# Two-block transformer kernel: the modulation's context sums by one VectorE instruction each

## The chip, the cores and the metric

One core of one Trainium2 chip runs the whole program; nothing is shared with other cores. The metric is the time of one execution in microseconds (us) of device time. The engines are named as in the profile: PE is TensorE's matmuls and PEld its weight loads, DVE is VectorE, ACT is ScalarE, POOL is GpSimd and SP is the engine whose queue issues most transfers.

## The reference, cut to what matters

The input passes through two blocks of two layers each. The first block has in each layer a gated feed-forward network, an attention mixer and a second such network; the second block has attention over image and context tokens and a feed-forward network. What the change touches is the modulation of the second block. For each of its two layers `l`, two vectors of 1024 numbers (the silu of `c` and the silu of `c_ctx`) are multiplied by one matrix:

```
sc = jax.nn.silu(c)
sc_ctx = jax.nn.silu(c_ctx)
mod   = split_cols((sc     @ w_mod[l] + b_mod[l])[:, None, :], (D_MODEL,) * N_MOD)
mod_x = split_cols( sc_ctx @ w_mod[l] + b_mod[l],              (D_MODEL,) * N_MOD)
```

`w_mod[l]` is 1024 x 6144 in float32, 25 MB a layer. Both products need only the inputs, so they can be computed at any time before the second block uses them.

## The kernel before, in words

**Main work.** Everything large is a matmul in three passes (`mm3`, lines 335 to 343): weights and activations are each split into a rounded high part and a rest, and high by high, low by high and high by low are added up in PSUM. The weights come as 539 tiles of 128 x 1024 float32, in the order in which they are used (class `Weights`). Each tile is loaded by SP's queue into one of 3 staging buffers (`wst`, line 274). ScalarE copies it to a rounded high part (`whi`, line 295) and VectorE subtracts that from the tile to get the rest (`wlo`, line 296). There are 4 buffers each of `whi` and `wlo`, and a tile is split 4 tiles ahead of its use (line 305). A tile holds 8 blocks of 128 x 128, so it feeds 24 matmuls.

**The feed-forward layers of the first block** (`ffn1_layer`, lines 871 to 912). An up phase has 22 steps; each multiplies two blocks of columns (48 matmuls, two weight tiles), then VectorE scales the result (896) and multiplies it by its silu (899), and ScalarE and VectorE split the product for the next phase (347, 348). A down phase has 8 steps of 66 matmuls, each with an eviction by VectorE (830), and the input of the next layer split by ScalarE (542) and VectorE (543) while POOL adds up squares (556). After each step of either phase `self.step()` (350) takes one step of every background generator. What a background step issues is tied behind the step's last split and last matmul, so that it does not come ahead of these in the queues. The order of each engine's queue beyond that is set when the program is built, by a scheduler that works through a simulated time line.

**The modulation** (`mod_gen`, lines 722 to 796) is such a generator. It runs beside the first three feed-forward layers for layer 0 (`w_mod` in 6 chunks of 1024 columns, two chunks to each feed-forward layer), and beside the feed-forward network of the second block's first layer for layer 1 (12 chunks of 512 columns). For a chunk, 8 tiles `mw` of 128 x CW are loaded one after another by SP's queue (737). For each, `n` sums are kept in `macc`: number 0 belongs to `c` and number 1 to the context. The tile times one of the 16 columns of `sc` (a number for each partition) is added to its sum. For the first tile ScalarE writes both products (751). For the other seven, number 0 is multiplied and added by VectorE in one instruction (753). Number 1 is multiplied by ScalarE into a buffer `mp` (756, two buffers), and POOL adds that to `macc` (757). In layer 1 number 1 is only needed for 4 of the 12 chunks. Then ones-matmuls on TensorE add over the partitions (769), and the rows go by DRAM to where they are used. This makes 6 x 7 = 42 additions of 1024 columns and 4 x 7 = 28 of 512 columns for number 1, and 42 and 12 x 7 = 84 for number 0.

Beside the second feed-forward layer another generator (`later_gen`, line 464) prepares constants by VectorE (479 to 524) and with two small matmuls (483, 509).

Of the kernel before, what the change touches and what calls it, by code (L numbers as in the profile page):

```python
# [8 lines left out]
FT = mybir.dt.float32  # L9
FR = mybir.dt.float32r  # L10
I32 = mybir.dt.int32
AF = mybir.ActivationFunctionType
OP = mybir.AluOpType
# [296 lines left out]
class Body:  # L310
# [411 lines left out]
    def mod_gen(self, pool, l, c0, c1, CW, nb, wait=0):  # L722

        nc = self.nc
        for _ in range(wait):
            yield
        gs = list(range(c0, c1, CW))
        if l:
            gs = gs[4:8] + gs[:4] + gs[8:]
        todo = [(g, k) for g in gs for k in range(KB)]  # L730
        ws = []

        def load():
            if todo:
                g, k = todo.pop(0)
                ws.append(pool.tile([128, CW], FT, name="mw", bufs=nb))
                nc.sync.dma_start(ws[-1], self.a["wmod"][l, k * 128:(k + 1) * 128, g:g + CW])

        for _ in range(nb - 1):
            load()  # L740
        yield
        for g in gs:
            n = 2 if l == 0 or g < 2 * D else 1
            acc = pool.tile([128, 2, CW], FT, name="macc")
            for k in range(KB):
                load()
                w = ws.pop(0)
                for i in range(n):
                    s = self.sc[:, i * 8 + k:i * 8 + k + 1]
                    if k == 0:  # L750
                        nc.scalar.activation(acc[:, i], w, AF.Copy, scale=s)
                    elif i == 0:
                        nc.vector.scalar_tensor_tensor(acc[:, i], w, s, acc[:, i], op0=OP.mult, op1=OP.add)  # L753
                    else:
                        t = pool.tile([128, CW], FT, name="mp", bufs=2)
                        nc.scalar.activation(t, w, AF.Copy, scale=s)  # L756
                        nc.gpsimd.tensor_tensor(acc[:, i], acc[:, i], t, op=OP.add)  # L757
                if CW == 1024 or k == KB - 1:
                    yield
                if CW == 1024 and k in (2, 5):  # L760
                    yield
            yield
            if CW == 1024:
                yield
            w = CW * n // 4
            rows = [(i, c) for i in range(n) for c in range(0, CW, w)]
            ps = self.ps("st")
            for p, (i, c) in enumerate(rows):
                nc.tensor.matmul(ps[32 * p:32 * p + 32, :w], self.ones[:, :32], acc[:, i, c:c + w], start=True,
                                 stop=True, tile_position=(0, 32 * p), skip_group_check=True)  # L770
            mr = self.w2(1)[:, 0, :w]
            nc.scalar.activation(mr, ps[:, :w], AF.Copy)
            for p, (i, c) in enumerate(rows):
                nc.sync.dma_start(self.rowd[l][i:i + 1, g + c:g + c + w], mr[32 * p:32 * p + 1])
            yield
        if c1 == 6 * D:
            mt = pool.tile([128, CW], FT, name="mt", tag="mp", bufs=2)[:96, :128]
            if n == 2:
                nc.sync.dma_start(mt, self.rowd[l].rearrange("i (k c) -> (i k) c", c=128))
            else:  # L780
                nc.vector.memset(mt, 0.0)
                nc.sync.dma_start(mt[:48], self.rowd[l][0:1].rearrange("i (k c) -> (i k) c", c=128))
                nc.sync.dma_start(mt[48:64], self.rowd[l][1:2, :2048].rearrange("i (k c) -> (i k) c", c=128))
            yield
            ps = self.ps("st")
            nc.tensor.transpose(ps[:, :96], mt, self.ident[:96, :96])
            b = self.vec[:, _VEC["b_mod"] + 48 * l:_VEC["b_mod"] + 48 * l + 48]
            mv = self.modv[l].rearrange("p (i c) -> p i c", i=2)
            nc.vector.tensor_tensor(mv, ps[:, :96].rearrange("p (i c) -> p i c", i=2),
                                    b[:, None, :].to_broadcast([128, 2, 48]), op=OP.add)  # L790
            for half in range(2):
                c = 24 * half + 16
                nc.vector.tensor_scalar(mv[:, :, c:c + 8], mv[:, :, c:c + 8], 1.0 / ALPHA, None, op0=OP.mult)
                nc.vector.tensor_scalar(self.s1p[l][:, :, half], mv[:, :, 24 * half + 8:24 * half + 16], 1.0, None,
                                        op0=OP.add)
            yield
# [1262 lines left out]
```

## Time and profile before

| What | us |
|---|---|
| median of 3 runs | 2051.03 |
| lowest and highest of them | 2048.58, 2056.51 |
| the profiled execution, whole | 2053.4 |
| its span, first to last instruction | 2051.6 |

The profiled execution is one run beside the three. Its time is the span and 1.8 us around it. Times in the rows are counted from the start of the span. A row's time for an instruction runs from its start to its end and includes what it was held up in between; the time that its engine stood idle ahead of it is given apart, with what released it. On TensorE matmuls overlap, so the starts are 0.12 us apart where one lasts 0.28. A time of POOL is rougher than the others.

### The profile page before, as it was taken

The numbers are of one execution on the slowest core, as the hardware profiler recorded it, in microseconds if no ns is written. First come the engines' busy times: TensorE is split into PE (matmuls) and PEld (weight loads), VectorE is DVE, ScalarE is ACT, GpSimd is POOL, SyncE is SP. The second block draws the span as 40 slices with busy tenths as digits, with TensorE's granted clock in tenths as the row PEclk, the third lists the DMA queues.
The fourth block names the chain that finished last, engine by engine and source line by source line (L and its number), as shares of the span: only waits on it lengthen the run. The fifth ranks groups of instructions, "written<-read, shape, count | busy, mean of one in ns | idle before, by whom it ended". The sixth has DMA issues, their size and how long they took to land. (4 is left out here: it accounts for less than half of the span.)

```text
span 2051.6 us, 39230 instructions
## 1 busy us (share of the span) xinstructions
PE 1985.8 (97%) x15365; PEld 1849.7 (90%) x15365; DVE 1525.1 (74%) x2683; ACT 1134.9 (55%) x2030; POOL 401.3 (20%) x305
## 2 busy tenths in 40 slices
PE   8998999998999999999999999999999999989997
PEld 8998999997999998999999777988888889869997
DVE  6887797988588867887686977766665689876554
ACT  5464586654466557555557765533443455855443
POOL 1222141312022310210430112302330014011002
PEclk9999999999999999999999999999999999999999
DMA  7775645785677663555542323475455653125553
GB/s 261 244 258 174 197 143 185 257 275 174 225 232 234 193 208 105 194 174 186 188 139 71 113 71 121 151 248 173 159 161 167 218 162 105 54 78 164 181 181 102
DMA packets 117689, 355.39 MB, mean 173 GB/s; under 512 B 21973, under 2 KB 28328, under 8 KB 117056
## 3 DMA queue, kind: packets, MB, share of 16 engines
q1 hardware_dynamic: 115904, 344.54, 51.8%
q10 hardware_dynamic: 1600, 8.36, 1.1%
q8 instruction: 120, 1.97, 0.4%
q14 instruction: 65, 0.53, 0.1%
HBM read 351.66 MB, written 8.90 MB: 176 GB/s over the span
## 5 line engine op out<-in xcount | busy, mean ns | idle before, releaser
L296 DVE TENSOR_TENSOR wlo<-wst,whi 128x1024 fp32r<-128x1024 f32 (+1 forms) x542 | 708.1, 1307 | 329.7 <-ACT whi L295 325.7
L341 PE MATMUL mm<-HI,whi 128*128 128x256 f32 (+1 forms) x2944 | 862.8, 295 | 6.8 <-ACT whi L295 2.6
L343 PE MATMUL mm<-HI,wlo 128*128 128x256 f32 (+1 forms) x2944 | 861.8, 294 | 5.8 <-DVE wlo L296 5.8
L342 PE MATMUL mm<-LO,whi 128*128 128x256 f32 (+1 forms) x2944 | 863.3, 294 | 1.5 <-DVE LO L1446 1.5
L295 ACT ACTIVATE whi<-wst 128x1024 fp32r<-128x1024 f32 (+1 forms) x542 | 569.9, 1053 | 512.4 <-PE mm L342 263.3
L341 PEld LDWEIGHTS mm<-HI,whi 128*128 128x128 f32 x2944 | 561.7, 192 | 31.1 <-issue 11.0
L343 PEld LDWEIGHTS mm<-HI,wlo 128*128 128x128 f32 x2944 | 563.5, 192 | 22.3 <-DVE wlo L296 7.4
L342 PEld LDWEIGHTS mm<-LO,whi 128*128 128x128 f32 x2944 | 564.0, 192 | 18.9 <-issue 6.0
L343 PE MATMUL mm<-ghi,wlo 128*128 128x256 f32 (+1 forms) x1000 | 290.0, 290 | 8.0 <-DVE wlo L296 8.0
L341 PE MATMUL mm<-ghi,whi 128*128 128x256 f32 (+1 forms) x1000 | 289.1, 290 | 1.6 <-ACT ghi L347 1.6
L342 PE MATMUL mm<-glo,whi 128*128 128x256 f32 (+1 forms) x1000 | 289.3, 290 | 0.6 <-DVE glo L348 0.6
L757 POOL TENSOR_TENSOR macc<-macc,mp 128x1024 f32<-128x1024 f32 (+1 forms) x70 | 162.6, 2323 | 479.5 <-ACT mp L756 332.3
L343 PEld LDWEIGHTS mm<-ghi,wlo 128*128 128x128 f32 x1000 | 193.3, 193 | 12.2 <-DVE wlo L296 8.8
L341 PEld LDWEIGHTS mm<-ghi,whi 128*128 128x128 f32 x1000 | 193.0, 193 | 6.4 <-issue 3.1
L342 PEld LDWEIGHTS mm<-glo,whi 128*128 128x128 f32 x1000 | 193.3, 193 | 3.5 <-issue 1.1
L753 DVE SCALAR_TENSOR_TENSOR macc<-mw,sc,macc 128x512 f32<-128x512 f32 (+1 forms) x126 | 175.1, 1389 | 25.1 <-DMA mw<-in_wmod 19.3
L342 PE MATMUL mm<-wlo,HI 128*128 128x256 f32 x352 | 100.5, 286 | 3.5 <-DVE wlo L296 3.5
L341 PE MATMUL mm<-whi,HI 128*128 128x256 f32 x352 | 100.9, 287 | 0.0
L343 PE MATMUL mm<-whi,LO 128*128 128x256 f32 x352 | 99.9, 285 | 0.0
L756 ACT ACTIVATE mp<-mw,sc 128x1024 f32<-128x1024 f32 (+1 forms) x70 | 67.1, 973 | 27.2 <-DMA mw<-in_wmod 18.0
L898 ACT ACTIVATE w<-w 128x256 f32<-128x256 f32 x88 | 36.1, 412 | 74.4 <-DVE w L896 73.0
L342 PEld LDWEIGHTS mm<-wlo,HI 128*128 128x128 f32 x352 | 67.5, 192 | 4.9 <-DVE wlo L296 4.1
(428 smaller groups left out, 2480.7 us busy)
## 6 DMA issues: line engine op xcount, KB each, us to landing
wst<-in_wall SPq DMA_DIRECT2D x539, 512.0 KB
mw<-in_wmod SPq DMA_DIRECT2D x48, 512.0 KB
mw<-in_wmod SPq DMA_DIRECT2D x96, 256.0 KB
brep<-bvec ACTq DMA_DIRECT2D x16, 384.0 KB
nab<-rrep SPq DMA_DIRECT2D x24, 96.0 KB
bias<-brep SPq DMA_DIRECT2D x4, 512.0 KB
bias<-brep SPq DMA_DIRECT2D x8, 256.0 KB
rrep<-in_rpb ACTq DMA_DIRECT2D x4, 348.8 KB
```

Source lines behind the costliest of these rows:

```text
L295: mark = self.nc.scalar.activation(hi[:, a:b], src[:, a:b], AF.Copy)
L296: self.nc.vector.tensor_tensor(lo[:, a:b], src[:, a:b], hi[:, a:b].bitcast(FT), op=OP.subtract)
L341: nc.tensor.matmul(ps, wh, xh, start=first, stop=False, skip_group_check=True)
L342: nc.tensor.matmul(ps, wh, xl, start=False, stop=False, skip_group_check=True)
L343: self.last = nc.tensor.matmul(ps, wl, xh, start=False, stop=last, skip_group_check=True)
L753: nc.vector.scalar_tensor_tensor(acc[:, i], w, s, acc[:, i], op0=OP.mult, op1=OP.add)
L756: nc.scalar.activation(t, w, AF.Copy, scale=s)
L757: nc.gpsimd.tensor_tensor(acc[:, i], acc[:, i], t, op=OP.add)
L898: nc.scalar.activation(sl, t[:, 0], AF.Silu)
```

## The change

For the second to eighth tile, both sums are now formed by VectorE's instruction that multiplies by a column and adds; the ScalarE product, its buffer and the POOL addition of number 1 are gone. The first tile's products stay on ScalarE. Loads, buffers of `mw` and `macc`, the generator's steps and the ones-matmuls stay as they are.

```diff
--- before.py
+++ after.py
@@ -749,12 +749,8 @@
                     s = self.sc[:, i * 8 + k:i * 8 + k + 1]
                     if k == 0:
                         nc.scalar.activation(acc[:, i], w, AF.Copy, scale=s)
-                    elif i == 0:
+                    else:
                         nc.vector.scalar_tensor_tensor(acc[:, i], w, s, acc[:, i], op0=OP.mult, op1=OP.add)
-                    else:
-                        t = pool.tile([128, CW], FT, name="mp", bufs=2)
-                        nc.scalar.activation(t, w, AF.Copy, scale=s)
-                        nc.gpsimd.tensor_tensor(acc[:, i], acc[:, i], t, op=OP.add)
                 if CW == 1024 or k == KB - 1:
                     yield
                 if CW == 1024 and k in (2, 5):
```

## Rows read from the trace of the kernel before

**Rows 1.** The page, part 1: busy time of each engine over the whole execution.

```profile
...
PE 1985.8 (97%) x15365; PEld 1849.7 (90%) x15365; DVE 1525.1 (74%) x2683; ACT 1134.9 (55%) x2030; POOL 401.3 (20%) x305
...
```

**Rows 2.** Busy time by stretch: us, engines' busy us (instructions), granted clock, DMA share, GB/s.

```profile
...
40.00:215.00 175.00, 167.41 (x1343) 161.90 (x1343) 143.33 (x144) 96.10 (x128) 44.66 (x20) 0.98 0.68 227
360.00:530.00 170.00, 160.52 (x1316) 157.76 (x1315) 143.62 (x191) 93.65 (x125) 41.15 (x18) 0.99 0.71 234
560.00:735.00 175.00, 173.68 (x1442) 171.31 (x1441) 147.36 (x150) 100.83 (x135) 46.40 (x19) 1.00 0.67 215
1330.00:1650.00 320.00, 319.35 (x1860) 270.37 (x1859) 203.64 (x255) 125.30 (x181) 44.20 (x28) 1.00 0.58 188
...
166.40:173.20 6.80, 5.47 (x25) 5.48 (x26) 6.80 (x6) 3.86 (x5) 2.73 (x2) 0.50 0.45 152
...
487.30:490.50 3.20, 3.20 (x17) 3.20 (x16) 2.63 (x4) 3.20 (x5) 1.17 (x1) 0.50 0.71 195
...
```

**Rows 3.** Waits of TensorE, 40 to 735 us: total us, times, longest.

```profile
...
PE mm L343 <- DVE wlo L296: 11.9, 7, 3.3
PE st L509 <- DVE w L499: 4.1, 1, 4.1
PE mm L341 <- ACT ghi L347: 1.6, 1, 1.6
...
```

**Rows 4.** The page, part 5: the POOL additions and the ScalarE products.

```profile
...
L757 POOL TENSOR_TENSOR macc<-macc,mp 128x1024 f32<-128x1024 f32 (+1 forms) x70 | 162.6, 2323 | 479.5 <-ACT mp L756 332.3
...
L756 ACT ACTIVATE mp<-mw,sc 128x1024 f32<-128x1024 f32 (+1 forms) x70 | 67.1, 973 | 27.2 <-DMA mw<-in_wmod 18.0
...
```

**Rows 5.** Timeline of VectorE, 157 to 169.5 us: start, us, engine, line, operation.

```profile
...
157.58 6.82 DVE L753 SCALAR_TENSOR_TENSOR macc<-mw,sc,macc 128x1024 f32<-128x1024 f32 x2
164.32 3.35 DVE L296 TENSOR_TENSOR wlo<-wst,whi 128x1024 fp32r<-128x1024 f32 x1
...
167.93 1.27 DVE L753 SCALAR_TENSOR_TENSOR macc<-mw,sc,macc 128x1024 f32<-128x1024 f32 x1
169.12 1.21 DVE L296 TENSOR_TENSOR wlo<-wst,whi 128x1024 fp32r<-128x1024 f32 x1
...
```

**Rows 6.** Timeline of POOL over the same stretch.

```profile
...
157.56 9.03 POOL L757 TENSOR_TENSOR macc<-macc,mp 128x1024 f32<-128x1024 f32 x3 [6.00 <-ACT mp L756]
...
```

**Rows 7.** Line 753 alone: instructions, shortest/median/longest in ns.

```profile
...
L753 DVE SCALAR_TENSOR_TENSOR macc<-mw,sc,macc x126: 737/754/3505, 48.1 to 1630.3; 128x512 f32<-128x512 f32 x84, 128x1024 f32<-128x1024 f32 x42
...
```

**Rows 8.** Groups of VectorE by shape, 40 to 215 us: busy us, mean ns, idle before.

```profile
...
L296 DVE TENSOR_TENSOR wlo<-wst,whi 128x1024 fp32r<-128x1024 f32 x56 | 78.3, 1401 | 26.1 <-ACT whi L295 26.1
L753 DVE SCALAR_TENSOR_TENSOR macc<-mw,sc,macc 128x1024 f32<-128x1024 f32 x14 | 30.8, 2200 | 0.0
...
```

**Rows 9.** Groups of VectorE by shape, 360 to 530 us.

```profile
...
L296 DVE TENSOR_TENSOR wlo<-wst,whi 128x1024 fp32r<-128x1024 f32 x54 | 73.8, 1368 | 24.4 <-ACT whi L295 24.4
L753 DVE SCALAR_TENSOR_TENSOR macc<-mw,sc,macc 128x1024 f32<-128x1024 f32 x14 | 33.2, 2371 | 0.0
...
L497 DVE TENSOR_SCALAR w<-vec,nbb 128x8 f32<-128x8 f32 x3 | 5.0, 1682 | 0.0
...
```

**Rows 10.** Groups of VectorE by shape, 560 to 735 us.

```profile
...
L296 DVE TENSOR_TENSOR wlo<-wst,whi 128x1024 fp32r<-128x1024 f32 x60 | 86.7, 1445 | 25.9 <-ACT whi L295 25.7
L753 DVE SCALAR_TENSOR_TENSOR macc<-mw,sc,macc 128x1024 f32<-128x1024 f32 x14 | 30.8, 2203 | 0.0
...
```

**Rows 11.** Groups of VectorE by shape, 1330 to 1650 us.

```profile
...
L753 DVE SCALAR_TENSOR_TENSOR macc<-mw,sc,macc 128x512 f32<-128x512 f32 x84 | 80.2, 955 | 25.1 <-DMA mw<-in_wmod 19.3 <-ACT macc L751 4.6
...
```

**Rows 12.** Groups of VectorE by shape, 149 to 170 us.

```profile
...
L753 DVE SCALAR_TENSOR_TENSOR macc<-mw,sc,macc 128x1024 f32<-128x1024 f32 x4 | 11.5, 2878 | 0.0
L296 DVE TENSOR_TENSOR wlo<-wst,whi 128x1024 fp32r<-128x1024 f32 x4 | 7.0, 1750 | 1.4 <-ACT whi L295 1.4
...
```

**Rows 13.** Groups of VectorE by shape, 464 to 499 us.

```profile
...
L753 DVE SCALAR_TENSOR_TENSOR macc<-mw,sc,macc 128x1024 f32<-128x1024 f32 x5 | 13.0, 2593 | 0.0
...
```

**Rows 14.** Timeline of TensorE, 160 to 168.5 us: start, us, operation, idle before.

```profile
...
167.72 0.58 PE L343 MATMUL mm<-ghi,wlo 128*128 128x256 f32 x1 [3.27 <-DVE wlo L296]
...
```


## The prediction

> **What bounds the kernel now.** I first read the busy times of the page [rows 1]: PE is busy 1985.8 of 2051.6 us, so TensorE is the bound, and another engine matters only where TensorE waits for it. VectorE, which gets the new work, is at 1525.1 us (74%), and that is an average over stages. So I read next the four stretches in which the modulation runs [rows 2]. The reader is to see that TensorE idles 175 - 167.41 = 7.6 us in the first, 9.5 in the second, 1.3 in the third and 0.6 in the fourth: 18.4 us in the three of layer 0, almost nothing in layer 1. VectorE is busy 82 to 85% of the first three and 64% of the fourth. Two short stretches run at half the clock, 6.8 us from 166.4 and 3.2 us from 487.3 [rows 2].
>
> Then I asked what TensorE waited for between 40 and 735 us [rows 3]: 11.9 us in 7 waits for the rest part of a weight tile (`wlo`, line 296), 4.1 us for one small constant (line 499), 1.6 us for ScalarE's split. The first two are 16.0 of the 18.4 us, and both are VectorE being late. Why it is late stands in its timeline [rows 5] beside POOL's [rows 6]. Alone, a sum of 1024 columns takes 1.27 us and a `wlo` 1.21. But the two sums that began at 157.58, just behind POOL's addition at 157.56, took 6.82 us, and the `wlo` behind them, while POOL still added, 3.35. POOL's three additions ran for 9.03 us in one row. So while POOL adds to `macc`, such a VectorE instruction stands still until the addition is over: (6.82 - 2.54) / 2 = 2.14 us a sum, 2.14 us for the `wlo`. The additions of the context sums are off TensorE's path, yet they hold up the engine that feeds it.
>
> **The change part by part.** It removes 70 products on ScalarE (67.1 us) and 70 additions on POOL (162.6 us) [rows 4], and adds 70 sums on VectorE.
>
> *Added.* 42 sums of 1024 columns; queued, one ends 1.19 us behind the other (167.93 to the next start at 169.12 [rows 5]): 14 to a stretch, 14 x 1.19 = 16.7 us each. 28 sums of 512 columns in layer 1: the median of line 753 is 0.754 us, and with 84 of its 126 of that shape that is the undisturbed short one [rows 7]: at most 21 us.
>
> *Removed from VectorE* is the standstill. First stretch [rows 8]: sums 30.8 - 14 x 1.27 = 13.0, `wlo` 78.3 - 56 x 1.21 = 10.5, together 23.5. Second [rows 9]: 15.4 + 8.5, and line 497, 5.0 us for three instructions of eight columns, of which I call 4.6 held up: 28.5. Third [rows 10]: 13.0 + 14.1 = 27.1. Against 16.7 added, VectorE gets 6.8, 11.8 and 10.4 us lighter: one engine doing both sums is quicker than the same engine doing one and standing still for the other. In layer 1 the sums lose 80.2 - 84 x 0.754 = 16.9 us [rows 11] and gain 21: about even, and TensorE waits only 0.6 us there. I put layer 1 at nothing; its cover is VectorE's slack of 36%.
>
> *What of that TensorE gets.* Only what lies in the queue ahead of one of its waits. From 149 to 170 us [rows 12] the four sums lose 11.5 - 5.1 = 6.4 and the `wlo` 7.0 - 4.8 = 2.2, and three or four added ones cost 3.6 to 4.8: 4 to 5 us less. The same burst against the lead: a tile is split four ahead, and feeds 24 matmuls at 173.68 / 1442 = 0.12 us [rows 2], so three tiles cover 8.7 us. The burst from 157.58 to 167.7 is 10 us long and overran it; with five sums and one `wlo` it is 5 x 1.19 + 1.21 = 7.2 and fits. With 1.4 us for the stretch's earlier wait (2.14 + 1.6 lost, two sums added) I take 5.4 of the 7.6 us. From 464 to 499 us [rows 13] the five sums lose 13.0 - 6.4 = 6.6, the two held-up 497s 4.6, and five added sums cost 6.0: 5.3 of the 9.5 us. In the third stretch the two sums and the `wlo` ahead of the only wait lose more than its 1.3 us. Sum 5.4 + 5.3 + 1.3 = 12.0 us. From above this is bounded by all 18.4, from below by the loss that the last rival gives, since no row excludes that the queue's new order brings new waits.
>
> *The clock.* The dip at 166.4 us came while TensorE stood in its longest wait for `wlo`, 3.27 us up to 167.72 [rows 14]. TensorE was busy for 5.47 us of it [rows 2], at 1.2 instead of 2.4 GHz, which cost half of that, 2.7. I count that as gained, since the wait goes. The other dip (3.2 / 2 = 1.6 us) followed the wait for the constant, much of which stays, and I let it stay. Bounds 0 and 4.3, taken 2.7.
>
> *Edits at nothing.* ScalarE loses work between its `whi` copies, which are ahead of `wlo`: no cost. SP's queue issues `mw` and `wst` in one line, and a load of `mw` waits for the tile's last reader. That was the sum or the product, and is now the second sum: 2.46 us after the first begins, where a held-up sum took 3.4 and a free one 1.27, so a `wst` behind it is up to 1.2 us later at times and 0.9 earlier at others. Three staged tiles cover that. The ones-matmuls now wait for VectorE alone, no longer for POOL, which ended later. The squares on POOL (556) no longer queue behind the additions. The program's order is set by the build's simulated time line and can shift anywhere; I know no row for that, and allow 4 us either way.
>
> A rule against the change: the Trainium skill, Perfetto Trace Analysis, "Optimizing Scalar/DVE Operations", says that where DVE is saturated, offloading some work to Scalar or even GPSIMD may make sense; it adds that GPSIMD and DVE share an SBUF read port, so that shifting between those two may not help. By its first half the sum would be that of the last rival below, 2070. The standstill of 2.14 us in this trace is the second half, and by that it is the sum that follows.
>
> The profiled execution took 2053.4 us, its span and 1.8 around it: 2053.4 - 12.0 - 2.7 = 2038.7. The median of the runs is 2.4 lower, which would give 2036.3. I say **2037 us**, 0.7% less.
>
> **The rivals.** *All of it goes.* Every wait in the three stretches ends and no dip is left: 18.4 + 4.3 = 22.7 us, 2031 (2028 from the median). For it: VectorE gets lighter by 6.8, 11.8 and 10.4 us where TensorE idles 7.6, 9.5 and 1.3, and ScalarE's copies come sooner. Against: the constants of the second stretch still queue behind sums. Chance 0.18.
>
> *The order eats it.* VectorE's queue puts pairs of sums ahead of a `wlo` where one stood, so the waits shrink by less than half: at most 6 us and no dip gone, about 2047 (2053.4 - 6). For it: bursts exist in which several sums stand in a row, as at 157.58. Against: a pair, 2.46 us, is shorter than one held-up sum, 3.41. Chance 0.20.
>
> *VectorE becomes the bound.* The relief falls where TensorE doesn't wait, and the added sums fall into the bursts ahead of a `wlo`. With the seven waits on `wlo` [rows 3] each longer by two sums, 7 x 2.4 = 17 us: 2070. It decides where a run of sums and splits exceeds the lead of 8.7 us, that is with six sums or more in a row ahead of one `wlo`. For it: VectorE is at 82 to 85% there [rows 2], and 16.7 us more without relief would be 91 to 94%. Against: the relief is larger than the addition in every stretch [rows 8 to 10]. Chance 0.09.
>
> **How the numbers follow.** My forecast has 0.53, the rivals 0.18, 0.20 and 0.09. A measurement of this kernel can tell 0.5%, 10 us, from no change. Faster by more than that are most of the forecast (0.48) and the first rival (0.18), with a little of the second: 0.67. Within it: the rest of the forecast and nearly all of the second, 0.24. Slower by more: the last, 0.09. The range for 8 in 10 goes from the first rival with 2 us of the order's shift, 2026, to the second with 4 to 5, 2052; within my forecast alone it is 2030 to 2044.
>
> **What would show it.** After the change POOL should have no row in `macc`, no sum of 1024 columns or `wlo` beside the modulation should last over 1.3 us except beside POOL's squares, and VectorE's busy time should fall by some 25 us although it does 70 sums more. TensorE should idle about 6 us in the three stretches together, mostly for line 499, and the dip at 166 us should be gone. I am wrong if VectorE's busy time rises, if `wlo` still lasts over 3 us there, or if the idle time of the three stretches stays near 18 us while all that holds.

## The result, and the profile after

The kernel after takes **2028.49 us** (median of 4 runs, 2027.52 to 2030.82) against 2051.07 before: 0.9885 of it, interval 0.987 to 0.990. In a second comparison it was 2030.44 against 2049.49, ratio 0.990 (0.9886 to 0.9914). Its profiled execution took 2030.8 us with a span of 2028.9, so against the profiled execution of before 22.6 us went. The prediction was 2037, in a range from 2026 to 2052. The direction and the mechanism were right; the time lies below the 2030 to 2044 of the forecast alone and came out at the rival called "All of it goes" (2028 to 2031), which the range had been drawn to take in.

The busy times of the page, to be read against [rows 1]:

```profile
...
PE 1982.3 (98%) x15365; PEld 1848.0 (91%) x15365; DVE 1489.9 (73%) x2753; ACT 1072.3 (53%) x1960; POOL 240.6 (12%) x235
...
```

VectorE does 70 instructions more and is busy for 35 us less; POOL has lost 161 us and ScalarE 63. The four stretches (columns as in [rows 2]):

```profile
...
40.00:215.00 175.00, 175.00 (x1430) 169.77 (x1430) 138.87 (x165) 85.75 (x120) 7.23 (x6) 1.00 0.73 237
360.00:530.00 170.00, 170.00 (x1416) 168.06 (x1415) 137.94 (x209) 82.75 (x116) 6.06 (x6) 1.00 0.77 254
560.00:735.00 175.00, 175.00 (x1454) 172.95 (x1454) 136.23 (x166) 86.23 (x122) 6.26 (x8) 1.00 0.69 222
1330.00:1650.00 320.00, 316.22 (x1847) 265.15 (x1847) 196.00 (x305) 107.45 (x160) 7.75 (x6) 0.99 0.57 180
...
```

TensorE is now busy for every microsecond of the three stretches of layer 0, where it idled for 18.4. In the fourth, 316.22 of 320 is not a new wait beside the modulation: the window ends at 1650, and all after the third stretch now comes some 23 us sooner, so that it takes in the start of the next stage; from 1330 to 1640 us TensorE is busy for 310.00 of 310. TensorE's waits from 30 to 735 us (as [rows 3]) are down to two small ones of the attention part:

```profile
...
PE half L996 <- DVE LO L1006: 1.0, 1, 1.0
PE tp L989 <- DVE r L983: 0.4, 1, 0.4
...
```

And VectorE's groups from 40 to 215 us, against [rows 8]:

```profile
...
L296 DVE TENSOR_TENSOR wlo<-wst,whi 128x1024 fp32r<-128x1024 f32 x60 | 73.1, 1221 | 31.6 <-ACT whi L295 31.4
L753 DVE SCALAR_TENSOR_TENSOR macc<-mw,sc,macc 128x1024 f32<-128x1024 f32 x28 | 34.8, 1278 | 0.0
...
```

28 sums take 34.8 us where 14 took 30.8. Each is 1.28 us, and a `wlo` 1.22: neither is held up any more. Line 543 still is, beside POOL's squares (0.85 us on the mean there). Between 40 and 735 us no wait of TensorE for VectorE beside the modulation is left, neither for `wlo` nor for the constant of line 499.

### The profile page after: what moved, and what is told of

Same layout as the page of the kernel before. It is cut to its first block, busy times and chain, and to the rows that moved or that the text cites. A ratio compares the mean times of both kernels' runs of the same rounds, so it can differ in the third digit from the quotient of the medians.

```text
span 2028.9 us, 39038 instructions
## 1 busy us (share of the span) xinstructions
PE 1982.3 (98%) x15365; PEld 1848.0 (91%) x15365; DVE 1489.9 (73%) x2753; ACT 1072.3 (53%) x1960; POOL 240.6 (12%) x235
## 5 line engine op out<-in xcount | busy, mean ns | idle before, releaser
L296 DVE TENSOR_TENSOR wlo<-wst,whi 128x1024 fp32r<-128x1024 f32 (+1 forms) x542 | 670.2, 1238 | 333.0 <-ACT whi L295 330.0
L753 DVE SCALAR_TENSOR_TENSOR macc<-mw,sc,macc 128x512 f32<-128x512 f32 (+1 forms) x196 | 185.0, 975 | 22.9 <-DMA mw<-in_wmod 17.9
L556 POOL TENSOR_TENSOR sacc<-sacc,w 128x256 f32<-128x256 f32 x36 | 34.7, 965 | 616.0 <-ACT w L552 614.9
L341 PEld LDWEIGHTS mm<-whi,HI 128*128 128x128 f32 x352 | 68.4, 195 | 1.2 <-ACT HI L1441 0.9
L343 PEld LDWEIGHTS mm<-whi,LO 128*128 128x128 f32 x352 | 68.1, 194 | 1.4 <-DVE LO L1442 0.9
```

What stands on the lines that cost most here:

```text
L296: self.nc.vector.tensor_tensor(lo[:, a:b], src[:, a:b], hi[:, a:b].bitcast(FT), op=OP.subtract)
L341: nc.tensor.matmul(ps, wh, xh, start=first, stop=False, skip_group_check=True)
L343: self.last = nc.tensor.matmul(ps, wl, xh, start=False, stop=last, skip_group_check=True)
L556: nc.gpsimd.tensor_tensor(st["acc"], st["acc"], sq, op=OP.add)
```

## The experiments

Each run stands beside runs of the kernel before on the same chip. Ratios are to these, with 95% intervals.

### POOL's and ScalarE's work kept, into a tile that nothing reads

```diff
+            idle = pool.tile([128, CW], FT, name="midle")
...
                         nc.vector.scalar_tensor_tensor(acc[:, i], w, s, acc[:, i], op0=OP.mult, op1=OP.add)
+                    if k and i:
+                        t = pool.tile([128, CW], FT, name="mp", bufs=2)
+                        nc.scalar.activation(t, w, AF.Copy, scale=s)
+                        nc.gpsimd.tensor_tensor(idle, t if k == 1 else idle, t, op=OP.add)
```

> The kernel after, with the ScalarE products and the POOL additions of before issued as well, into a tile that nothing reads. Theory (standstill: a VectorE instruction with its inputs in SBUF cannot run while POOL adds): the kernel after gained because POOL stopped, so with POOL adding again the gain goes. VectorE then has both the 16.7 us of added sums in each of the three stretches and a standstill of over 20 us: slower than before, 2055 to 2090 us, TensorE idle for more than 18 us in the three stretches, sums of 1024 columns near 2.2 us each on the mean. Rival (hand-over: the gain comes from the chain ScalarE, POOL, sum, ones-matmul being one engine's now): nothing waits for the tile, so about 2028 to 2032 us.

Measured: 2087.73 us, ratio 1.0179 (1.0163 to 1.0195). The stretches, then VectorE's sums from 0 to 800 us, POOL's additions there (36 of 42; the first of each chunk has other operands), and TensorE's waits from 30 to 735:

```profile
...
40.00:215.00 175.00, 162.34 (x1260) 156.37 (x1259) 155.20 (x153) 90.37 (x119) 46.43 (x18) 0.95 0.65 216
360.00:530.00 170.00, 159.63 (x1264) 156.74 (x1263) 158.02 (x196) 92.57 (x124) 40.91 (x16) 0.96 0.67 225
560.00:735.00 175.00, 164.10 (x1290) 160.01 (x1290) 155.35 (x155) 93.20 (x124) 42.12 (x16) 0.96 0.60 194
...
```

```profile
...
L754 DVE SCALAR_TENSOR_TENSOR macc<-mw,sc,macc 128x1024 f32<-128x1024 f32 x84 | 165.4, 2006 | 0.0
...
```

```profile
...
L758 POOL TENSOR_TENSOR midle<-midle,mp 128x1024 f32<-128x1024 f32 x36 | 106.9, 2971 | 214.1 <-ACT mp L757 213.8
...
```

```profile
...
PE mm L343 <- DVE wlo L296: 16.9, 12, 3.7
PE mm L342 <- DVE glo L348: 8.0, 4, 2.6
PE mm L341 <- ACT whi L295: 4.2, 2, 3.4
...
```

TensorE idles for 12.7, 10.4 and 10.9 us, and its clock is granted at 0.95 to 0.96. A sum takes 2.0 us on the mean where it took 1.28 without POOL. Nothing reads what POOL adds here, so no hand-over can be late: what was put back costs by running. The hand-over rival falls. That it is POOL's additions and not ScalarE's products, which were put back too, is for the next run to tell.

### VectorE adds the product, ScalarE still makes it

```diff
-                        nc.gpsimd.tensor_tensor(acc[:, i], acc[:, i], t, op=OP.add)
+                        nc.vector.tensor_tensor(acc[:, i], acc[:, i], t, op=OP.add)
```

> The kernel before, with the addition of the product moved from POOL to VectorE; the 70 ScalarE products of 67 us and their buffers stay. Theory (standstill): POOL no longer adds, and VectorE's added instruction is about as long as the sum of the kernel after, so nearly the whole gain: 2027 to 2034 us. Rival (ScalarE: the gain comes from the 67 us of products that no longer stand between ScalarE's copies of weight tiles): the products are still there, so 2040 to 2052 us.

Measured: 2029.78 us, ratio 0.9896 (0.9882 to 0.9911), the time of the kernel after within the spread. VectorE's groups from 0 to 800 us:

```profile
...
L753 DVE SCALAR_TENSOR_TENSOR macc<-mw,sc,macc 128x1024 f32<-128x1024 f32 x42 | 53.6, 1277 | 0.0
L757 DVE TENSOR_TENSOR macc<-macc,mp 128x1024 f32<-128x1024 f32 x42 | 51.0, 1215 | 0.0
...
```

The product's addition (line 757) takes 1.22 us, like the sum that replaces it in the change. All 70 products are still on ScalarE. So the gain is that of moving the addition off POOL; taking the products off ScalarE, and doing both in one instruction, gives nothing here that can be measured.

### POOL's additions in pieces of 256 columns

```diff
-                        nc.gpsimd.tensor_tensor(acc[:, i], acc[:, i], t, op=OP.add)
+                        for q in range(0, CW, 256):
+                            r = slice(q, q + 256)
+                            nc.gpsimd.tensor_tensor(acc[:, i, r], acc[:, i, r], t[:, r], op=OP.add)
```

> The kernel before, with each POOL addition issued as pieces of 256 columns (four for 1024, two for 512). Theory (standstill for one whole POOL instruction at a time): a piece takes about 0.9 us by the squares' additions of that size, so a VectorE instruction is held up for at most about 0.9 us by one piece, if it then goes ahead of the next. Sums of 1024 columns fall from 2.26 us on the mean to 1.6 to 2.0, and the time to 2035 to 2047 us. If pieces follow so closely that VectorE cannot go in between, the sums stay at 2.2 us or more and the time at 2051 or above. Rival (ScalarE, or hand-over): 2051 us or more, whatever the sums take, since every product and hand-over is still there.

Measured: 2035.21 us, ratio 0.992 (0.9903 to 0.9937). VectorE from 0 to 800 us, then POOL:

```profile
...
L296 DVE TENSOR_TENSOR wlo<-wst,whi 128x1024 fp32r<-128x1024 f32 x250 | 327.3, 1310 | 126.3 <-ACT whi L295 123.0 <-PE mm L343 2.0 <-PE mm L342 0.7
L753 DVE SCALAR_TENSOR_TENSOR macc<-mw,sc,macc 128x1024 f32<-128x1024 f32 x42 | 72.1, 1717 | 0.1
...
```

```profile
...
L759 POOL TENSOR_TENSOR macc<-macc,mp 128x256 f32<-128x256 f32 x168 | 216.1, 1318 | 228.1 <-ACT mp L756 228.1
...
```

POOL's rows add up to more than before: 216.1 us up to 800 us alone, where all 70 additions of the whole run took 162.6 [rows 4]. Yet three quarters of what the second experiment gave come (0.8 of 1.04%): the sums fall from 2.26 us on the mean (30.8 + 33.2 + 30.8 us for 42 [rows 8 to 10]) to 1.72, and a `wlo` takes 1.31 from 0 to 800 us where it was 1.36. So POOL's working time is not what costs; VectorE's standstill is. By these means against the shapes alone (1.28 and 1.22 us) it falls from some 75 to 41 us up to 800 us. Whether shorter stops would help at the same sum was not tried.

### The stretches one by one

The change in one stretch alone, each by one condition:

```diff
-                    elif i == 0:
+                    elif i == 0 or (l == 0 and c0 == 0):
```

with `c0 == 2 * D` for the second stretch, `c0 == 4 * D` for the third, and `l == 1` for layer 1.

First:

> The change in the first feed-forward layer's two chunks alone; the other stretches as before. By the idle time of the kernel before (7.6 us, and 2.7 us for the clock dip behind it), 2051 - 10.3 = 2040.8: 2038 to 2044 us, with the second stretch still idle for about 9.5 us. Rival (a new order of the queues over the whole program makes the gain): the other stretches change as well, and the time falls by well over 10 us or hardly at all.

Second:

> The change in the second feed-forward layer's two chunks alone. Theory (each stretch's idle time is its own, and all of it goes): 9.5 us and 1.6 us for the dip, so 2051 - 11.1 = 2040: 2037 to 2043 us, with the wait for the constant of line 499 gone too. Rival (as in the prediction: the relief within the stretch's own backlog, 5.3 us, with the constant's wait staying): 2044 to 2048 us.

Third:

> The change in the third feed-forward layer's two chunks alone. Theory (each stretch gives its own idle time): 1.3 us, so 2047 to 2051 us where before is 2050.4. Rival (the stretches' gains don't add up, since the first two alone gave 8 to 9 us each of a total near 23): 4 us or more, 2043 to 2046.

Layer 1:

> The change in layer 1's chunks of 512 columns alone. Theory (a standstill of VectorE costs only where TensorE waits for it): TensorE idles for 0.6 us there, so the same as before within 0.2%, 2047 to 2055 us, though the sums fall from 0.95 to 0.75 us on the mean. Rival (all relief of VectorE counts): up to 17 us less, 2034 to 2045 us.

Measured: first 2043.16 us, ratio 0.9958 (0.9941 to 0.9975); second 2042.17, 0.9960 (0.9947 to 0.9974); third 2048.51, 0.9994 (0.9982 to 1.0006); layer 1 2050.62, 1.0001 (0.999 to 1.0012). The first two stretches with the change in the first, then with it in the second:

```profile
...
40.00:215.00 175.00, 175.00 (x1428) 169.57 (x1427) 138.21 (x165) 85.71 (x119) 6.84 (x6) 1.00 0.71 236
360.00:530.00 170.00, 166.15 (x1357) 163.80 (x1356) 142.78 (x194) 94.89 (x125) 42.35 (x19) 0.98 0.73 245
...
```

```profile
...
40.00:215.00 175.00, 168.63 (x1351) 163.12 (x1350) 142.87 (x145) 96.68 (x128) 44.68 (x20) 0.98 0.67 227
360.00:530.00 170.00, 170.00 (x1416) 168.06 (x1416) 138.72 (x212) 83.82 (x118) 5.71 (x5) 1.00 0.75 254
...
```

The changed stretch is without idle time in both. Of the others, the second keeps 3.9 us in the first run, where I had expected about 9.5, and the first keeps 6.4 in the second run; how much a stretch idles varies from run to run, since with layer 1 alone changed it is 5.6 us in each. By the ratios the stretches give 8.6, 8.2 and 1.2 us, 18.0 together, against 20.5 and 23.6 for the whole change in two comparisons; the intervals overlap, so no gain beyond the sum of the stretches is shown. The third stretch's 1.2 us is not clear of noise. Layer 1 is the clearest case. VectorE from 1280 to 1650 us with the change there alone:

```profile
...
L753 DVE SCALAR_TENSOR_TENSOR macc<-mw,sc,macc 128x512 f32<-128x512 f32 x112 | 80.7, 746 | 21.2 <-DMA mw<-in_wmod 16.4 <-ACT macc L751 4.1
...
```

A sum falls from 0.955 us [rows 11] to 0.75, POOL's 44 us there [rows 2] go, and the time is the same: TensorE did not wait there.

### The constant's matmul one step later

```diff
                 nc.vector.tensor_copy(lc[:, :, 5], w[:, :, 1])
                 yield
+                yield
```

> The kernel before, with the small matmul of line 509 one background step later; nothing else. Theory A (VectorE is late by its own backlog, and TensorE meets that at whatever stands next in its queue): the wait of 4.1 us for the constant goes, but the following waits for wlo grow by about as much, and the time stays within 2 us of before, 2048 to 2054 us. Theory B (only the place of that matmul was at fault): the 4.1 us and the clock dip behind it go, 2043 to 2047 us.

Measured: 2050.32 us, ratio 0.9998 (0.9986 to 1.0010). TensorE's waits from 30 to 735 us:

```profile
...
PE mm L343 <- DVE wlo L296: 6.4, 4, 3.3
PE mm L341 <- ACT ghi L347: 3.5, 2, 3.1
...
```

The wait for line 499 is gone, and by the runs nothing is gained: Theory A stands by the time. The trace shows what TensorE met instead (VectorE, then TensorE):

```profile
...
473.06 2.46 DVE L497 TENSOR_SCALAR w<-vec,nbb 128x8 f32<-128x8 f32 x1
...
```

```profile
...
480.48 0.58 PE L341 MATMUL mm<-ghi,whi 128*128 128x256 f32 x1 [3.11 <-ACT ghi L347]
...
```

In both kernels line 497 is held up, 2.44 us before and 2.46 here, ahead of what TensorE needs next. Before, that was line 499, and TensorE waited for 4.1 us; here it is `ghi`, which ScalarE makes from a product that VectorE forms behind line 497, and TensorE waits for 3.1. The clock dip stays as well: it is granted at 0.50 from 480.4 to 484 us. So the place of that matmul was not what cost the 4.1 us: VectorE was late there, and TensorE met that at what stood next in its queue. I had expected `wlo` to take the wait over, and it was `ghi`; the waits for `wlo` are shorter here than before, 6.4 us against 11.9, but this profile is of the fastest of ten runs (2044.4 us), and why is open.

### Other POOL work, after the change

The kernel after was run again on the chip of the run on the squares and of the last run below.

> The kernel after, unchanged, beside the next three on one chip: 2026 to 2031 us, and a spread of its runs of at most 5 us where the kernel before has 11, if the waits on VectorE are also what makes the kernel before vary from run to run.

Measured: 2030.44 us, four runs from 2029.43 to 2031.43. The kernel before spread from 2045.06 to 2054.73 in 17 runs there and from 2044.91 to 2056.07 in 21 runs of the comparison ahead of it. Fewer waits go with less spread, as far as four runs tell; that the waits are the cause is not shown.

Squares:

```diff
-            nc.gpsimd.tensor_tensor(st["acc"], st["acc"], sq, op=OP.add)
+            nc.vector.tensor_tensor(st["acc"], st["acc"], sq, op=OP.add)
```

> The kernel after, with the additions of squares of line 556 (36 of 256 columns, of about 1 us on POOL) moved to VectorE. They too hold up VectorE (line 543 takes 0.68 us on the mean in place of 0.48), but in the three stretches TensorE no longer waits for anything. Theory (a standstill costs only ahead of a wait): the same as after within 0.15%, 2025 to 2031 us. Rival (POOL off is always better): 2018 to 2024 us.

Measured: 2029.54 us, 0.9 us below the kernel after on the same chip (2028.58 to 2029.89 against 2029.43 to 2031.43), within the 0.15%. VectorE's line 543 from 0 to 800 us is no longer held up (0.48 us where it took 0.69), and the time gains nothing from it:

```profile
...
L543 DVE SCALAR_TENSOR_TENSOR LO<-h,vec,HI 128x256 fp32r<-128x256 f32 x42 | 19.7, 478 | 5.2 <-ACT HI L542 5.1
...
```

The additions to the bias tiles, the norms' subtractions and the multiplications behind them:

```diff
-                    nc.gpsimd.tensor_tensor(d, d, self.cst[...], op=OP.add)
+                    nc.vector.tensor_tensor(d, d, self.cst[...], op=OP.add)
...
-            nc.gpsimd.tensor_tensor(dst[:, s], src[:, s], b(mu), op=OP.subtract)
+            nc.vector.tensor_tensor(dst[:, s], src[:, s], b(mu), op=OP.subtract)
...
-            self.nc.gpsimd.tensor_tensor(T[:, s], T[:, s], rms[...], op=OP.mult)
+            self.nc.vector.tensor_tensor(T[:, s], T[:, s], rms[...], op=OP.mult)
```

> The kernel after, with three more kinds of POOL instructions moved to VectorE: the additions to the bias tiles (line 1881), the subtractions of the mean in the norms (1262) and the multiplications that follow (1514). They run at one place, from 1000 to 1016 us, where VectorE's sums, products and wlo beside them last 1.2 to 2.3 us instead of 0.7 to 1.2 and TensorE then waits 1.7 and 1.9 us. Theory (standstill): VectorE does them in less than it stood still; TensorE's two waits shrink, 1 to 4 us less than after, 2024 to 2028 us. Rival (here VectorE is the path itself, so what it takes over adds up): 2029 to 2036 us.

Measured: **2024.36 us** (2023.02 to 2026.93), ratio 0.9879 (0.9863 to 0.9894). It did not run beside the kernel after, only beside the kernel before. In the kernel after, VectorE, POOL and TensorE's waits at that place:

```profile
...
1001.71 2.99 DVE L1266 TENSOR_TENSOR h<-ex,w 128x512 f32<-128x512 f32 x2
1004.62 4.64 DVE L1267 TENSOR_TENSOR h<-h,rstd 128x512 f32<-128x512 f32 x3
...
1010.89 2.30 DVE L296 TENSOR_TENSOR wlo<-wst,whi 128x1024 fp32r<-128x1024 f32 x1
...
```

```profile
...
1002.41 3.45 POOL L1262 TENSOR_TENSOR h<-ex,w 128x512 f32<-128x512 f32 x2
1008.67 6.96 POOL L1514 TENSOR_TENSOR ex<-ex,rstd 128x512 f32<-128x512 f32 x4
...
```

```profile
...
PE mm L342 <- DVE wlo L296: 3.3, 2, 1.8
...
```

And VectorE there with all of it on VectorE:

```profile
...
1002.60 1.28 DVE L1262 TENSOR_TENSOR h<-ex,w 128x512 f32<-128x512 f32 x2
1003.80 1.28 DVE L1266 TENSOR_TENSOR h<-ex,w 128x512 f32<-128x512 f32 x2
...
1007.29 1.22 DVE L296 TENSOR_TENSOR wlo<-wst,whi 128x1024 fp32r<-128x1024 f32 x1
1008.42 2.49 DVE L1267 TENSOR_TENSOR h<-h,rstd 128x512 f32<-128x512 f32 x4
1010.83 2.50 DVE L1514 TENSOR_TENSOR ex<-ex,rstd 128x512 f32<-128x512 f32 x4
...
```

Two subtractions of line 1266 take 1.28 us in place of 2.99, four multiplications of line 1267 2.49 where three took 4.64, the `wlo` 1.22 in place of 2.30. TensorE's wait for `wlo` there, 3.3 us in both profiles of the kernel after, is gone. This version beats the kernel before. Against the kernel after it is 4 to 6 us lower by the medians of two other comparisons, and 1 to 4 us by the ratios to the kernel before, whose intervals overlap. So the 3.3 us of this place are read from the traces; that this version is the faster of the two is likely, but its times do not show it.

The norms' other POOL instructions (31 multiplications and 16 subtractions), on top of the edit above:

```diff
-            nc.gpsimd.tensor_tensor(T[:, s], R[:, s], sw[...], op=OP.mult)
+            nc.vector.tensor_tensor(T[:, s], R[:, s], sw[...], op=OP.mult)
...
-                nc.gpsimd.tensor_tensor(R[:, s], R[:, s], rm[...], op=op)
+                nc.vector.tensor_tensor(R[:, s], R[:, s], rm[...], op=op)
```

> The kernel of the eighth run, with the norms' other POOL multiplications (lines 1433 and 1463 after the change, 47 of 512 columns, 1.4 to 1.7 us each) on VectorE as well. They run beside the attention, where TensorE has waits of 1.4 us (1226 and 1243 us) and wlo is held up by 0.3 to 1.1 us at a time. Theory (standstill): on VectorE they take 0.7 us each, less than the standstill where the two meet, but 47 x 0.7 = 33 us of new work where they don't: 2020 to 2026 us. Rival (VectorE becomes the bound there): 2027 to 2040 us.

Measured: 2038.98 us (2038.16 to 2041.19), ratio 0.9944 (0.9930 to 0.9958), 13 to 15 us above the version before it and 8.5 above the kernel after on the same chip. My theory fell here, and the rival's time holds. TensorE's waits at the norms over the whole run, then the same waits in the version before it:

```profile
...
PE mm L342 <- DVE LO L1442: 5.3, 2, 3.6
PE tp L1423 <- DVE h L1439: 4.9, 1, 4.9
...
PE tp L1423 <- DVE h L1437: 2.7, 1, 2.7
...
```

```profile
...
PE tp L1423 <- DVE h L1439: 3.8, 1, 3.8
...
PE mm L342 <- DVE LO L1442: 1.2, 3, 0.4
...
PE tp L1423 <- DVE h L1437: 0.8, 1, 0.8
...
```

In the norms (lines 1437 to 1442) TensorE waits for VectorE's last products, 12.9 us where it was 5.8. One place on VectorE:

```profile
...
1820.35 1.90 DVE L1433 TENSOR_TENSOR h<-ex,sw 128x512 f32<-128x512 f32 x3 [2.22 <-ACT sw L1429]
...
1827.23 2.49 DVE L1463 TENSOR_TENSOR ex<-ex,w 128x512 f32<-128x512 f32 x4
...
```

The three products of line 1433, which had run on POOL beside VectorE's own (3.93 us from 1813.70 in the version before), now stand for 1.90 us ahead of line 1437, and TensorE's wait for that line grows by 1.9. The four of line 1463 stand ahead of a line 1442 that TensorE waits 3.6 us for. VectorE is not busier over the whole run (1486.1 and 1486.6 us); some of its work now stands at a worse place. The waits account for about half of the loss; the rest was not traced, and which of the two lines costs more was not tried.

## Why the prediction was right, and where it was short

*The bound and the mechanism:* right. TensorE was late for VectorE, and VectorE for POOL. The first three experiments tell it from a late hand-over and from ScalarE's load. The standstill is close to one whole POOL instruction at a time, 2.14 us by [rows 5] where a POOL addition that is not held up itself takes 2.40 (at 98.70 us). The Trainium skill, SBUF — State Buffer, "Who interferes with whom", says that a DVE instruction with two SBUF inputs contends with a GpSimd instruction that reads SBUF, over a shared pair of ports that is an exclusive lock, and that a DVE instruction with at most one SBUF input outside the 2-port modes does not. The runs agree: in the first experiment, with POOL adding, all 66 of line 897 up to 800 us (one operand in PSUM) take 0.67 to 0.69 us, as line 896 does in the kernel before.

*Added and removed on VectorE:* right in direction, 10 us short. I said 25 us lighter; it is 35.2 (1525.1 to 1489.9). The `wlo` give back 37.9 us over the run where I had 33.1 for the three stretches, the sums add 9.9 where I had 12.8, line 497 gives back 4.4 where I had 4.6, and lines 543 and 348, which I had left out, give back some 3.

*Layer 1 at nothing:* right, shown by the run of layer 1 alone.

*"What of that TensorE gets", 12.0 us:* this is the step that was too small. It measured 18.4. I counted, wait by wait, the relief in the queue just ahead of it, as if each microsecond there were a microsecond of waiting. But the tiles split ahead are a lead, and TensorE waits only once it is used up. A tile feeds TensorE for 2.9 us (24 x 0.12); each longer pause between two `wlo` eats of the lead, and pauses add up. This is how a wait in the kernel before came about (VectorE, then TensorE):

```profile
...
98.72 3.46 DVE L753 SCALAR_TENSOR_TENSOR macc<-mw,sc,macc 128x1024 f32<-128x1024 f32 x1
...
102.45 1.21 DVE L296 TENSOR_TENSOR wlo<-wst,whi 128x1024 fp32r<-128x1024 f32 x1
...
105.72 2.81 DVE L296 TENSOR_TENSOR wlo<-wst,whi 128x1024 fp32r<-128x1024 f32 x1
...
```

```profile
...
108.58 0.39 PE L343 MATMUL mm<-HI,wlo 128*128 128x256 f32 x1 [1.73 <-DVE wlo L296]
...
```

From the end of one `wlo` to the end of the next there are 5.2 us (98.5 to 103.7) and 4.9 (to 108.5), each far below the 8.7 us of the prediction, and yet TensorE waits for 1.7. Of the seven waits for `wlo` before, five came behind pauses of 4.9 to 8.2 us. So the 8.7 us, which reckon with one pause and the whole lead, do not tell when TensorE waits. Here is the longest pause of the first stretch in the kernel after (timeline of VectorE):

```profile
...
151.60 2.49 DVE L296 TENSOR_TENSOR wlo<-wst,whi 128x1024 fp32r<-128x1024 f32 x2
...
154.34 3.67 DVE L753 SCALAR_TENSOR_TENSOR macc<-mw,sc,macc 128x1024 f32<-128x1024 f32 x3
...
158.26 1.28 DVE L753 SCALAR_TENSOR_TENSOR macc<-mw,sc,macc 128x1024 f32<-128x1024 f32 x1
159.45 1.22 DVE L296 TENSOR_TENSOR wlo<-wst,whi 128x1024 fp32r<-128x1024 f32 x1
...
```

Four sums stand between the `wlo` that ends at 154.1 and the one that ends at 160.7: 6.6 us, where the longest pause before, with two held-up sums and a held-up `wlo` [rows 5], was 10.3 (157.3 to 167.7). It costs nothing at all. In the other two stretches the longest are now 5.9 and 6.9 us, where they were 9.9 and 8.2. With shorter pauses the lead was never used up in any of the three; the change in the second stretch alone leaves 170.00 of its 170 us busy. That every wait went is measured; that the lead decided it is read from these pauses, and no run changed the lead.

*The constant's wait, "much of which stays":* wrong, 4.1 us and the dip of 1.6 behind it. I thought that the sums ahead of it would keep it. After the change line 497 takes 0.22 to 0.23 us where it had taken up to 2.44, and no wait for line 499 is left. The run with the matmul one step later shows that the wait was VectorE's lateness there, met at that place.

*The clock:* the dips at 166.4 and 487.3 us are gone, as the granted clock of 1.00 in the three stretches shows. I had counted on 2.7 of the 4.3 us. With 18.4 that makes 22.7, and 22.6 were measured between the two profiled executions. That the two agree to 0.1 us is partly luck: each is one execution, 2.3 us above the median of its kernel, and in the runs that left these stretches unchanged TensorE idled 5.6 to 6.4 us in the first and 3.9 to 5.6 in the second, where the profile before has 7.6 and 9.5.

*SP's queue, the ones-matmuls and ScalarE at nothing:* TensorE waits for none of them in the three stretches. *The rival on the other side*, VectorE as the bound, did not come in this change. TensorE waited more for VectorE in the last experiment, with POOL work of another kind.

## What to carry to other kernels

Work put on GpSimd to relieve VectorE can load VectorE instead: look at the durations of VectorE's instructions beside GpSimd's, against the same shape alone, before you count such work as free. It costs time only where the pauses that it makes, one after another, use up what the bound engine has in its buffers; look for that engine's waits, not for the standstill. Taking such work back paid where such waits stood (18.4 us here; 3.3 more at the norm, by the trace), gave nothing where there were none (layer 1, squares), and lost where it put VectorE's added work ahead of products that TensorE waited for.

## What was not expected of the hardware

An instruction of eight columns (line 497, one input tile and a column) was held up as well: beside a POOL addition it took 2.44 and 2.38 us in the kernel before, without one 0.22 [rows 9 has the three together], though it does next to no work. And cutting a POOL instruction into four, which made POOL's rows longer in all, brought most of the gain: VectorE's sums were held up for less, 1.72 us on the mean where they had taken 2.26.
